# Eight changes of order in a hybrid encoder block: masks before gate casts, up casts after the last inverse, x loads after the gates', QKV low parts on VectorE, first MLP blocks in order

## The chip, the cores and the metric

The kernel runs on one core of a Trainium2 chip. A core has a matrix engine (TensorE, PE in the profile), a vector engine (VectorE, DVE), a scalar engine (ScalarE, ACT), a general engine (GpSimd, POOL) and SyncE (SP), which here only issues DMA transfers. Each engine works through its own list of instructions in order, and semaphores tie the lists together. The metric is the device time of one execution, in microseconds (us).

## The reference, cut to what matters

One layer, 1024 tokens, model width 1024, all in float32:

```python
h = rms_norm(x, norm_mix)
proj = h @ w_in                       # 768 columns QKV, 1792 RWKV, 2048 gates
q, k = rotary(rms_norm(q)), rotary(rms_norm(k))
attn = windowed_gqa(q, k, v, sink)    # 8 query heads, 2 key heads, +-128 tokens
rw   = rwkv7_time_mix(shifted(zr))    # a forward and a backward scan, summed
gates = sigmoid(proj[..., O_GATE:])   # one gate per branch and channel
merged = gates[0] * (attn @ w_up_attn) + gates[1] * (rw @ w_up_rwkv)
x = x + merged @ w_out
x = x + square(relu(rms_norm(x) @ w_ff1)) @ w_ff2
x = x + (p @ w_ple) * sigmoid(rms_norm(x) @ w_ple_gate)
```

The scan updates, for each of 8 heads and both directions, a 64 x 64 state at every token: `state * w + (state @ a) b^T + v k^T`, and reads it with `r`.

## The kernel before, in words

**Operands.** Every float32 operand of a large product is split in two by `split` (L196): a high part, cast by ScalarE (L201), and a low part, the remainder, by VectorE or GpSimd (L202). A product is then three matmuls: high by high, high by low, low by high. A weight block therefore goes through a load into a staging buffer, a cast and a subtraction before TensorE can use it. `load_w` (L213) does this for a block of 128 columns, here in two parts of 128x512.

**Order.** A planner gives each engine's instructions their order, from the program's order as a priority and its own simulation of when operands are there. `tc.keep_in_program_order` pins an instruction to the program's order; the helper `mmo` (L228) does so for a matmul and `turn` for VectorE's instructions of the recurrence. `after(ins, prev)` asks for one instruction to stand behind another on its engine.

**Stages.** First come the norm of x and the QKV projection, a token tile of 128 at a time. The eight weight rows of QKV are loaded and split by `load_wq`; the tuple `WQP` names those whose low part GpSimd makes, the others are VectorE's. `rotated(t)` (from L417 on) normalises and rotates queries and keys of a tile and casts them (L433, L438), and `heads(t)` transposes them (L404) and copies the result out of PSUM with ScalarE (`qkT`, L406). The heads of the last two tiles, `h6` and `h7`, are spread among the matmuls of the projection's next blocks.

Then come attention, the RWKV projections and half of the gates. The scan works in chunks of 64 tokens, 16 steps `s`, both directions at once. A step masks products of the chunk's operands (`gm`, L1192, by VectorE), solves with the inverse of a triangular matrix, and carries the state on. The inverses are made for a block of NB = 4 steps at a time while the steps of the block before it run: `inverse_steps` has 31 pairs of VectorE instructions (L1324, L1327) and a last turn with two transposes, `Zn` and `Zt` (L1331, L1332). A step takes as many of these 32 turns as the row of `TURNS` for its place in the block says, in three positions. `end_inverse` joins the quarter blocks at the end of every fourth step: TensorE's `qps` matmuls, ScalarE's copies `Q` and `zi` (L883, L884).

TensorE has gaps in a scan step, and the generator `beside` fills them: it yields one matmul at a time, of the gates of the second half of the tokens, then, after 16 empty yields (`BRIDGE`), of the lift of the attention branch (`uaps`). `fill(n)` takes n of them. What the generator emits between two yields, loads and splits among it, stands in the program where its step is taken. Before the lift it casts two weight blocks and four parts of the attention's output (`wuhi`, `aTh`). In the last `end_inverse`, behind step 11, the generator's steps are taken between the first and the second half of the `qps` matmuls, by `between`, and at once after.

Behind the scan the RWKV branch is lifted (`up_rwkv`, 8 blocks for each half of the tokens). For each block SyncE loads a gate tile `g1t` and the gated attention part `mgt`, and the next up weights, and at places of its list parts of `w_out` (`load_wo`) and the tiles of x. In the code before, four tiles of x (`x1a`) and the gain row `gainf` have no order asked for but the program's.

The output projection, the second norm and the MLP follow. The MLP multiplies in blocks with seven products each, whose operands are sums of blocks (`product`, L1664). Its first two row blocks (`p` of 0 and 1) begin before all of the sums are made. These matmuls are placed by the planner.

Of the kernel before, what the change touches and what calls it, by code (L numbers as in the profile page):

```python
# [17 lines left out]
P = 128  # L18
# [27 lines left out]
NAT = (0, 1)  # L46
WQP = (0, 2, 4)
WQPIN = 8
# [18 lines left out]
FILLQ = (9, 7)  # L67
TURNS = ((0, 0, 4), (3, 2, 5), (3, 2, 5), (4, 3, 1))

LOW_AT = (1, 2)  # L70
# [77 lines left out]
def block_kernel(ctx: ExitStack, tc: tile.TileContext, I: dict, out: bass.AP):  # L148
# [63 lines left out]

    def load_w(pl, tag, src, n, bufs=2, sbufs=2, lo_eng=None, stag=None, parts=1, stages=(), q=None):  # L213

        k = src.shape[1]
        hi = pl.tile([P, k, n], F32R, name="whi", tag=tag + "_hi", bufs=bufs)
        lo = pl.tile([P, k, n], F32R, name="wlo", tag=tag + "_lo", bufs=bufs)
        step = k // parts
        for i in range(0, k, step):
            spl, stg, sb = stages[(i // step) % len(stages)] if stages else (pl, stag or tag + "_st", sbufs)  # L220
            st = spl.tile([P, step, n], F32, name="wst", tag=stg, bufs=sb)
            (q or nc.sync).dma_start(st, src[:, i:i + step])
            split(hi[:, i:i + step], lo[:, i:i + step], st, lo_eng or nc.gpsimd)
        return hi, lo
# [103 lines left out]
    def gates(h, ms=range(2 * KT), mm=nc.tensor.matmul, lo_of=lambda m: nc.gpsimd):  # L328

        for m in ms:  # L330
            c0 = O_GATE + m * P
            hi, lo = load_w(PW, "w", w_col(c0), P, parts=2, lo_eng=lo_of(m), q=nc.gpsimd if (h, m) in GQ else None)
            ps = PMM.tile([P, 512], F32, name="gmm", tag="mm", bufs=2)
            yield from mm3_steps(ps, [(hi[:, k, :], lo[:, k, :], Hh[h][:, k, :], Hl[h][:, k, :]) for k in range(KT)], mm)
            th = PW.tile([P, 512], F32, name="gth", tag="gth", bufs=2)
            nc.scalar.activation(out=th, in_=ps, func=AF.Tanh, scale=0.5)
            epi["stored"] = nc.sync.dma_start(g_d[m, :, 512 * h:512 * h + 512], th)
            yield
# [4 lines left out]
    with ExitStack() as s0:  # L343
# [141 lines left out]
        for h in range(2):  # L485
            ps = PMM.tile([P, 512], F32, name="mm", tag="mm", bufs=2)
            z12.append(ps)
            for i, _ in enumerate(mm3_steps(ps, [(whl[0][:, k, :], whl[1][:, k, :], Hh[h][:, k, :], Hl[h][:, k, :]) for k in range(KT)])):
                if i % 6 == H6[0] and h == H6[1]:
                    next(h6, None)  # L490
            if h == 0:
                if H6[1] == 0:
                    for _ in h6:
                        pass
                rotated(NT - 1)
        for _ in h6:
            pass
        whl = load_w(PW, "w", w_col(O_RWKV + 1664), P, parts=2)
        z13 = []
# [504 lines left out]
    def beside():  # L1004
# [40 lines left out]

        ahead = [weights(0, sts[0])]
        for k in range(NP):
            part(k)
        load_at(1)
        ahead.append(weights(1, sts[1]))  # L1050
        for _ in range(BRIDGE):
            yield 1
# [123 lines left out]
    def products(s, hf):  # L1176
# [14 lines left out]
        for e in range(2):  # L1191
            turn(nc.vector.tensor_tensor(  # L1192
                out=gm[hf][:, s % NB, e].rearrange("p (a b) t -> p a b t", b=2), in0=pss[e][:, 0:6].rearrange("p (a b) t -> p a b t", b=2),
                in1=gmask.unsqueeze(2).broadcast_to([P, 3, 2, 64]), op=ALU.mult))

    def load_v(s):
# [180 lines left out]
    for s in range(NCH):  # L1377
# [28 lines left out]
        aside(0)  # L1406
        inverse_turn(TURNS[s % NB][0])
        gap(1)
# [3 lines left out]
        if more:  # L1412
            products(s + 2, 1)
        inverse_turn(TURNS[s % NB][1])
        gap(2)
# [7 lines left out]
        if first:  # L1423
            inv[0] = inverse_steps(s // NB + 1)
        inverse_turn(TURNS[s % NB][2])
        gap(5)
# [4 lines left out]
        if s % NB == NB - 1 and s // NB < 3:  # L1431
            end_inverse(s // NB + 1, lambda: fill(FILLQ[0]))
            fill(FILLQ[1])
        if s % NB or s // NB >= 3:
# [28 lines left out]
    def load_wo(n, ks, spl, tag, sbufs):  # L1463

        for k in ks:
            st = spl.tile([P, 2, 512], F32, name="wst", tag=tag, bufs=sbufs)
            nc.sync.dma_start(st, wov[:, k:k + 2, 512 * n:512 * n + 512])
            split(wo[n][0][:, k:k + 2], wo[n][1][:, k:k + 2], st, behind=None if n else epi["done"])

# [3 lines left out]
    for e in range(2):  # L1473
        mTh[e] = AC[e].tile([P, KT, 512], F32R, name=f"mh{e}", tag="ab0", bufs=1)
        mTl[e] = AC[e].tile([P, KT, 512], F32R, name=f"ml{e}", tag="ab1", bufs=1)

    def up_rwkv(m, e):

# [3 lines left out]
        mg = GP.tile([P, 2, 256], F32, name="mgt", bufs=3)  # L1482
        nc.sync.dma_start(mg, tset(mg_d[m], e))
        if (m + e) % 2:
# [74 lines left out]
    with ExitStack() as s7:  # L1559
# [14 lines left out]
        gainf = NR.tile([P, DM], F32, name="gainf", bufs=1)  # L1574
        nc.sync.dma_start(gainf, I["gains"][1:2, :].partition_broadcast(P))
        for i in (4, 5, 6, 7, 0, 1, 2, 3):
            t = torder[i]
            nc.sync.dma_start(x1[t], I["x"][t * P:(t + 1) * P, :])
            out_proj(i, 0)
# [78 lines left out]
    def product(ps, p, r, start=True):  # L1658
# [3 lines left out]
        for k in range(4):  # L1662
            for i, (x_, y_) in enumerate(((ah, bh), (ah, bl), (al, bh))):
                nc.tensor.matmul(ps, x_[:, k, :], y_[:, k, :], start=start and k + i == 0, stop=k == 3 and i == 2, skip_group_check=True)  # L1664

# [369 lines left out]
```

## Time and profile before

| what | value |
| --- | --- |
| median of 3 runs | 1653.21 us (1650.28 to 1654.63) |
| the profiled execution | 1652.3 us |
| its span in the profile | 1650.5 us, 31173 instructions |
| TensorE busy | 1601.0 us, 97% |
| VectorE busy | 1136.0 us, 69% |
| ScalarE busy | 840.0 us, 51% |
| GpSimd busy | 90.6 us, 5% |
| mean granted TensorE clock | 0.992 of full speed |

Times in the views are microseconds from the start of the span. A row of the timeline has start, duration, engine, source line, operation, output and inputs, shapes and a count; in brackets stands the idle time of the engine ahead of it and what ended that. A row of the waits has who waited and for whom, then the total, the number of times and the longest. A row of windows has the stretch, its length, each engine's busy time with a count of instructions (PE, PEld, DVE, ACT, POOL), the granted clock, the share of time that the DMA engines were busy and what they moved. SPq is SyncE's DMA queue; an SPq row is the issue of a transfer, not the transfer.

### The profile page before, as it was taken

Reading aid. Unit: us, or ns where it says so; the run is one execution under the profiler, and the core shown is the slowest. Engines: PE = TensorE matmul, PEld = TensorE weight load, DVE = VectorE, ACT = ScalarE, POOL = GpSimd, SP = SyncE. Lnnn points to the kernel's source line nnn. Section 1 sums busy time; section 2 is a strip of 40 time slices with the busy share of each in tenths; the row PEclk is TensorE's granted clock in tenths of the full one; section 3 lists DMA queues with packets and bytes.
Section 4 is the critical chain, followed back from the end, with each engine's and each line's share of the span. In section 5 each row is a group of like instructions: output and inputs, shape, how many; then the busy total and the mean of one; then the engine's idle time right before and its main releaser. Section 6 shows DMA issues by size and latency. Waiting matters only on the chain.

```text
span 1650.5 us, 31173 instructions
## 1 busy us (share of the span) xinstructions
PE 1601.0 (97%) x12280; PEld 1297.2 (79%) x12280; DVE 1136.0 (69%) x2071; ACT 840.0 (51%) x1533; POOL 90.6 (5%) x113
## 2 busy tenths in 40 slices
PE   7999999999999999899999999999999999999998
PEld 6987777776678778676788778888888888888887
DVE  5648998468929679787827877666658877675332
ACT  5548888378653554554305454444445445454221
POOL 3430000310000000000001000000000000000000
PEclk9999999999989999999999999999999999999999
DMA  6352555864475744468723254444459855564011
GB/s 224 86 154 83 173 173 178 263 189 141 136 192 175 225 138 149 148 194 268 242 76 116 79 190 141 147 159 149 161 189 336 266 181 180 171 196 143 35 42 39
DMA packets 199810, 269.23 MB, mean 163 GB/s; under 512 B 47728, under 2 KB 103920, under 8 KB 199664
## 3 DMA queue, kind: packets, MB, share of 16 engines
q1 hardware_dynamic: 188448, 249.95, 47.6%
q0 software_dynamic: 11072, 16.78, 3.8%
q8 instruction: 96, 1.57, 0.4%
q10 hardware_dynamic: 144, 0.52, 0.1%
q14 instruction: 50, 0.41, 0.1%
HBM read 186.45 MB, written 80.74 MB: 162 GB/s over the span
## 4 chain that ended last, share of the span: by engine, by line
PE 73%; DVE 9%; DMA 7%; ACT 6%; issue 4%; POOL 1%; SPq 0%; DVEq 0%; POOLq 0%; ACTq 0%
PE ff1ps L1664 16%; PE ff2ps L1916 16%; PE gmm L228 4%; PE plps L238 2%; PE plps L236 2%; PE plps L234 2%; PE mm L246 2%; PE mm L247 2%; PE mm L248 2%; PE mmo L248 1%; PE mmo L246 1%; PE mmo L247 1%; DMA wst<-in_w_col_dram 1%; PE gps L228 1%; PE uaps L228 1%
## 5 line engine op out<-in xcount | busy, mean ns | idle before, releaser
L1916 PE MATMUL ff2ps<-tl,sh 128*128 128x512 f32 x448 | 174.5, 390 | 0.4 <-DVE tl L202 0.4
L1916 PE MATMUL ff2ps<-th,sl 128*128 128x512 f32 x448 | 174.4, 389 | 0.0
L1916 PE MATMUL ff2ps<-th,sh 128*128 128x512 f32 x448 | 173.9, 389 | 0.0
L201 ACT CAST sh<-sst 128x512 fp32r<-128x512 f32 x109 | 67.8, 622 | 101.5 <-PE ff2ps L1916 46.3
L202 DVE TENSOR_TENSOR sl<-sst,sh 128x512 fp32r<-128x512 f32 x109 | 75.0, 688 | 46.4 <-ACT sh L201 46.1
L1664 PE MATMUL ff1ps<-mh,w1h 128*128 128x512 f32 x256 | 100.3, 392 | 2.0 <-ACT w1h L201 2.0
L1664 PE MATMUL ff1ps<-ml,w1h 128*128 128x512 f32 x256 | 99.9, 390 | 0.0
L1664 PE MATMUL ff1ps<-mh,w1l 128*128 128x512 f32 x256 | 99.6, 390 | 0.0
L1916 PEld LDWEIGHTS ff2ps<-tl,sh 128*128 128x128 f32 x448 | 84.1, 188 | 18.6 <-DVE tl L202 1.1
L201 ACT CAST whi<-wst 128x512 fp32r<-128x512 f32 x100 | 60.0, 618 | 75.3 <-DMA wst<-in_w_col_dram 31.9
L1916 PEld LDWEIGHTS ff2ps<-th,sh 128*128 128x128 f32 x448 | 84.0, 188 | 17.9 <-ACT th L201 0.3
L1916 PEld LDWEIGHTS ff2ps<-th,sl 128*128 128x128 f32 x448 | 84.1, 188 | 17.4
L201 ACT CAST w1h<-w1st 128x512 fp32r<-128x512 f32 x48 | 28.4, 620 | 105.5 <-DMA w1st<-in_w_ff_dram 66.0
L202 DVE TENSOR_TENSOR wlo<-wst,whi 128x512 fp32r<-128x512 f32 x88 | 58.7, 684 | 19.7 <-ACT whi L201 17.0
L185 POOL TENSOR_TENSOR rstd<-ms,neghalf 128x1 f32<-128x1 f32 x24 | 14.8, 616 | 1016.0 <-PE ff2ps L1916 573.4
L202 DVE TENSOR_TENSOR w1l<-w1st,w1h 128x512 fp32r<-128x512 f32 x48 | 31.7, 687 | 50.4 <-ACT w1h L201 50.4
L1664 PEld LDWEIGHTS ff1ps<-mh,w1h 128*128 128x128 f32 x256 | 48.1, 188 | 13.0 <-ACT w1h L201 2.9
L1664 PEld LDWEIGHTS ff1ps<-mh,w1l 128*128 128x128 f32 x256 | 48.1, 188 | 11.0 <-DVE w1l L202 0.9
L1664 PEld LDWEIGHTS ff1ps<-ml,w1h 128*128 128x128 f32 x256 | 48.1, 188 | 10.0
L1192 DVE TENSOR_TENSOR gm<-gps,gmask 128x384 f32<-128x384 f32 x64 | 32.6, 549 | 32.7 <-PE gps L228 32.7
L234 PE MATMUL gmm<-hh,whi 128*128 128x512 f32 x128 | 52.2, 408 | 2.1 <-ACT whi L201 2.1
L228 PE MATMUL gmm<-hh,wlo 128*128 128x512 f32 x128 | 54.2, 423 | 0.0
(406 smaller groups left out, 4508.6 us busy)
## 6 DMA issues: line engine op xcount, KB each, us to landing
tst<-in_w_ff_dram SPq DMA_DIRECT2D x80, 256.0 KB, 4.1
wst<-in_w_col_dram SPq DMA_DIRECT2D x76, 256.0 KB, 3.8
w1st<-in_w_ff_dram SPq DMA_DIRECT2D x32, 512.0 KB, 5.0
hid_S<-h SPq DMA_DIRECT2D x64, 256.0 KB, 2.1
sst<-hid_S SPq DMA_DIRECT2D x64, 256.0 KB, 3.3
hid_A<-h SPq DMA_DIRECT2D x48, 256.0 KB, 2.0
sst<-hid_A SPq DMA_DIRECT2D x45, 256.0 KB, 3.7
ra_d<-ra SPq DMA_DIRECT2D x8, 1024.0 KB, 6.4
```

The lines of the kernel that those rows point to most:

```text
L201: a = nc.scalar.copy(hi, src)
L202: b = (lo_eng or nc.vector).tensor_tensor(out=lo, in0=src, in1=hi.bitcast(F32), op=ALU.subtract)
L228: tc.keep_in_program_order(nc.tensor.matmul(*a, **kw))
L234: mm(ps, ah, bh, start=(i == 0), stop=False)
L236: mm(ps, ah, bl, start=False, stop=False)
L238: mm(ps, al, bh, start=False, stop=(i == n - 1))
L246: nc.tensor.matmul(ps, ah, bh, start=(i == 0), stop=False)
L247: nc.tensor.matmul(ps, ah, bl, start=False, stop=False)
L248: nc.tensor.matmul(ps, al, bh, start=False, stop=(i == n - 1))
L1192: turn(nc.vector.tensor_tensor(out=gm[hf][:, s % NB, e].rearrange("p (a b) t -> p a b t", b=2), in0=pss[e][:, 0:6].rearrange("p (a b) t -> ...
L1664: nc.tensor.matmul(ps, x_[:, k, :], y_[:, k, :], start=start and k + i == 0, stop=k == 3 and i == 2, skip_group_check=True)
L1916: nc.tensor.matmul(banks[bs][i], x_[:, isl], y_, start=fresh and p + j == 0, stop=p == NPR - 1 and j == 2, skip_group_check=True)
```

## The change

Eight edits, none of which adds or takes away a matmul:

1. `WQP` is emptied: VectorE makes all low parts of QKV weights.
2. A second table `TURNS2` sets the inverse's turns in steps 8 to 11. It has the same sum, with the last turn taken earlier in step 11.
3. The casts ahead of the attention's lift are traced once `epi["turned"]` is set, which is behind the last `end_inverse`; the number of empty yields stays 16, or more if that is later.
4. The low part of gate block 1 of the second half is ordered behind the mask products of `products(0, 1)`.
5. `rotated(NT - 1)` is traced behind all of tile 6's heads.
6. `load_wo` splits each row of a weight part alone (128x512 instead of 128x1024).
7. The first four x loads are each ordered behind one of the last four loads of `mgt`, the rest behind the x load before; `gainf` is loaded behind the last of them.
8. The matmuls of the first two row blocks of the MLP are pinned to the program's order.

```diff
-WQP = (0, 2, 4)
+WQP = ()
 TURNS = ((0, 0, 4), (3, 2, 5), (3, 2, 5), (4, 3, 1))
+TURNS2 = ((0, 0, 5), (3, 3, 5), (3, 3, 5), (4, 1, 0))
...
-            split(hi[:, i:i + step], lo[:, i:i + step], st, lo_eng or nc.gpsimd)
+            split(hi[:, i:i + step], lo[:, i:i + step], st, lo_eng or nc.gpsimd, behind=(None, behind))
...
+            hi, lo = load_w(PW, "w", w_col(c0), P, parts=2, lo_eng=lo_of(m), q=nc.gpsimd if (h, m) in GQ else None,
+                            behind=epi.get("gm") if (h, m) == (1, 1) else None)
...
-                rotated(NT - 1)
         for _ in h6:
             pass
+        rotated(NT - 1)
...
-        ahead = [weights(0, sts[0])]
-        for k in range(NP):
-            part(k)
-        load_at(1)
-        ahead.append(weights(1, sts[1]))
-        for _ in range(BRIDGE):
+        n = 0
+        while n < BRIDGE or "turned" not in epi:
+            if "turned" in epi and "parts" not in epi:
+                ahead = [weights(0, sts[0])]
+                for k in range(NP):
+                    part(k)
+                load_at(1)
+                ahead.append(weights(1, sts[1]))
+                epi["parts"] = True
+            n += 1
             yield 1
...
         for e in range(2):
-            turn(nc.vector.tensor_tensor(
+            a = (nc.vector.tensor_tensor(
...
+            turn(a)
+            if s == 0:
+                epi["gm"] = a
...
-        inverse_turn(TURNS[s % NB][0])
+        inverse_turn((TURNS2 if s // NB == 2 else TURNS)[s % NB][0])
...
             end_inverse(s // NB + 1, lambda: fill(FILLQ[0]))
+            if s // NB == 2:
+                epi["turned"] = True
             fill(FILLQ[1])
...
-            split(wo[n][0][:, k:k + 2], wo[n][1][:, k:k + 2], st, behind=None if n else epi["done"])
+            for j in range(2):
+                split(wo[n][0][:, k + j], wo[n][1][:, k + j], st[:, j], behind=None if n else epi["done"])
...
-        nc.sync.dma_start(mg, tset(mg_d[m], e))
+        upl.append(nc.sync.dma_start(mg, tset(mg_d[m], e)))
...
-        nc.sync.dma_start(gainf, I["gains"][1:2, :].partition_broadcast(P))
-        for i in (4, 5, 6, 7, 0, 1, 2, 3):
+        for j, i in enumerate((4, 5, 6, 7, 0, 1, 2, 3)):
             t = torder[i]
-            nc.sync.dma_start(x1[t], I["x"][t * P:(t + 1) * P, :])
+            a = nc.sync.dma_start(x1[t], I["x"][t * P:(t + 1) * P, :])
+            after(a, upl[12 + j] if j < 4 else xload)
+            xload = a
+            if i == 0:
+                after(nc.sync.dma_start(gainf, I["gains"][1:2, :].partition_broadcast(P)), upl[15])
...
-                nc.tensor.matmul(ps, x_[:, k, :], y_[:, k, :], start=start and k + i == 0, stop=k == 3 and i == 2, skip_group_check=True)
+                (mmo if p < 2 else nc.tensor.matmul)(ps, x_[:, k, :], y_[:, k, :], start=start and k + i == 0, stop=k == 3 and i == 2, skip_group_check=True)
```

More of the change, by code (lines that the diff above doesn't have):

```diff
@@ L211, in split, with load_w @@
         return a, b
-    def load_w(pl, tag, src, n, bufs=2, sbufs=2, lo_eng=None, stag=None, parts=1, stages=(), q=None):
+    def load_w(pl, tag, src, n, bufs=2, sbufs=2, lo_eng=None, stag=None, parts=1, stages=(), q=None, behind=None):
         k = src.shape[1]
@@ L331, in gates @@
             c0 = O_GATE + m * P
-            hi, lo = load_w(PW, "w", w_col(c0), P, parts=2, lo_eng=lo_of(m), q=nc.gpsimd if (h, m) in GQ else None)
+            hi, lo = load_w(PW, "w", w_col(c0), P, parts=2, lo_eng=lo_of(m), q=nc.gpsimd if (h, m) in GQ else None,
+                            behind=epi.get("gm") if (h, m) == (1, 1) else None)
             ps = PMM.tile([P, 512], F32, name="gmm", tag="mm", bufs=2)
@@ L1413, in block_kernel @@
             products(s + 2, 1)
-        inverse_turn(TURNS[s % NB][1])
+        inverse_turn((TURNS2 if s // NB == 2 else TURNS)[s % NB][1])
         gap(2)
@@ L1424, in block_kernel @@
             inv[0] = inverse_steps(s // NB + 1)
-        inverse_turn(TURNS[s % NB][2])
+        inverse_turn((TURNS2 if s // NB == 2 else TURNS)[s % NB][2])
         gap(5)
@@ L1475, in block_kernel @@
         mTl[e] = AC[e].tile([P, KT, 512], F32R, name=f"ml{e}", tag="ab1", bufs=1)
+    upl = []
     def up_rwkv(m, e):
```

## The prediction, made before the changed kernel was run

> **What bounds the kernel now.** I read the head of the page first, then the list of TensorE's waits, then the granted clock by stretches of the span, and last the order of time around each place that the diff touches.
>
> ```profile
> span 1650.5 us, 31173 instructions
> PE 1601.0 (97%) x12280; PEld 1297.2 (79%) x12280; DVE 1136.0 (69%) x2071; ACT 840.0 (51%) x1533; POOL 90.6 (5%) x113
> ...
> PE gps L228 <- DVE gm L1192: 3.0, 1, 3.0
> PE gps L228 <- ACT zi L884: 2.9, 1, 2.9
> PE mmc L248 <- DVE wlo L202: 1.8, 2, 0.9
> PE ff1ps L1664 <- ACT w1h L201: 2.0, 2, 1.5
> PE qtp L404 <- ACT qkT L406: 1.6, 1, 1.6
> ```
>
> TensorE is busy for 1601.0 of 1650.5 us, and the change takes no matmul away. So it can win only single waits (columns: total us, times, longest) and time in which TensorE ran at a lower clock, which the busy share hides. The next rows (start:end, us; busy us and count of PE, PEld, DVE, ACT, POOL; granted clock; DMA share; GB/s) show three such stretches, each behind one of those waits.
>
> ```profile
> 453.00:460.00 7.00, 6.08 (x46) 5.21 (x47) 2.35 (x5) 1.04 (x3) 0.54 (x1) 0.51 1.23 243
> 668.00:671.50 3.50, 3.50 (x84) 2.48 (x86) 2.75 (x5) 2.91 (x5) 0.00 (x0) 0.51 0.02 5
> 678.00:681.70 3.70, 3.70 (x85) 2.83 (x80) 3.70 (x9) 2.37 (x5) 0.00 (x0) 0.54 0.94 286
> ```
>
> Work of 6.08 us at a clock of 0.51 would take 3.1 at full clock: 2.9 us are lost there. In the same way 3.50 x 0.49 = 1.7 and 3.70 x 0.46 = 1.7. So a wait of 1.5 to 3.0 us costs about twice its length when such a stretch follows.
>
> **Start: QKV low parts by VectorE.**
>
> ```profile
> 8.79 2.34 POOL L202 TENSOR_TENSOR wql<-wqs,wqh 128x768 fp32r<-128x768 f32 x1 [0.78 <-ACT wqh L201]
> 11.16 0.33 SPq L355 DMA_DIRECT2D wqs<-in_w_qkv_dram  x1
> 11.37 0.96 DVE L202 TENSOR_TENSOR wql<-wqs,wqh 128x768 fp32r<-128x768 f32 x1
> 20.67 1.80 ACT L201 CAST wqh<-wqs 128x768 fp32r<-128x768 f32 x2 [3.70 <-DMA wqs<-in_w_qkv_dram]
> 22.55 0.44 PE L460 MATMUL psq<-wql,hh 128*128 128x384 f32 x1 [0.55 <-DVE wql L202]
> ```
>
> A low part takes POOL 2.34 us and VectorE 0.96. POOL ends the first at 11.13, and SyncE issues the next load into that staging buffer at 11.16. VectorE would do it behind its work of that moment, and I estimate the load 0.65 earlier. The last weights reach TensorE at 22.55, after 3.70 us of ScalarE's waiting for DMA, so an earlier load can show there. Bounds: 0 (the queue is full of x and weights, and POOL's three parts, 2.9 us of VectorE, delay a norm there) to 1.4 (2.34 - 0.96). I take **0.65**.
>
> **The last query/key tile behind the heads of the tile before it.**
>
> ```profile
> 106.99 0.62 ACT L433 CAST q<-qn 128x512 fp32r<-128x512 f32 x1 [6.10 <-DVE qn L430]
> 107.91 1.06 ACT L406 CAST qkT<-qtp 128x512 fp32r<-128x512 f32 x2
> 108.54 0.66 PE L404 MATMUL qtp<-ident,k 128*128 128x128 f32 x4 [1.58 <-ACT qkT L406]
> ...
> 108.50:112.00 3.50, 3.46 (x20) 2.92 (x20) 0.92 (x4) 2.21 (x4) 1.89 (x3) 1.00 0.60 167
> ```
>
> ScalarE stands 6.10 us in front of tile 7's q cast, and the eviction that TensorE wants is queued behind it, to 107.91. With `rotated(7)` traced last, that eviction no longer has the cast in front. The clock behind this gap stays at 1.00, so nothing is added for it. Bounds 0 (tile 7's heads, a block of matmuls later, come late instead: their q cast moves behind all of tile 6's evictions) to 1.58. I take **1.6**.
>
> **The gates' low part behind the masks (block 1 of half 1).**
>
> ```profile
> 449.22 1.38 DVE L873 COPY zi<-Zt 32x1024 f32<-32x1024 f32 x2
> 451.20 0.69 DVE L202 TENSOR_TENSOR wlo<-wst,whi 128x512 fp32r<-128x512 f32 x1 [0.60 <-ACT whi L201]
> 452.71 0.69 DVE L202 TENSOR_TENSOR wlo<-wst,whi 128x512 fp32r<-128x512 f32 x1 [0.81 <-ACT whi L201]
> 453.32 1.01 DVE L1192 TENSOR_TENSOR gm<-gps,gmask 128x384 f32<-128x384 f32 x2
> 453.92 2.01 PE L228 MATMUL gps<-rac,bkc 64*64 64x128 f32 x32 [3.03 <-DVE gm L1192]
> ```
>
> VectorE is free at 449.22 + 1.38 = 450.60, yet it stands in two low parts that wait for their casts, and the masks start 2.7 us later. Put first, the two masks run to about 451.6 and the low parts follow; TensorE still stands about 0.7, so the wait falls by 2.3, and the stretch behind it regains 2.9: **5.2**, bounds 2.0 (clock kept low, the low part then late for its gate block) and 5.9 (all of 3.03 and 2.9). What the added order holds back are the two low parts, and behind them the gate block's matmuls; these wait for the masks at most their 1.0 us.
>
> **More inverse steps early, and casts behind the last inverse.**
>
> ```profile
> 630.72 0.32 DVE L1327 TENSOR_TENSOR Z<-Z,tmp 128x156 f32<-128x156 f32 x1
> ...
> 664.00 2.13 DVE L1331 STREAM_TRANSPOSE Zn<-Z 128x1024 f32<-128x1024 f32 x1
> 665.95 2.06 DVE L1332 STREAM_TRANSPOSE Zt<-Z 128x1024 f32<-128x1024 f32 x1
> 666.28 1.28 PE L228 MATMUL qps<-Zn,lt 32*32 32x32 f32 x128 [1.47 <-DVE Zn L1331]
> 673.84 0.61 ACT L201 CAST wuhi<-wust 128x512 fp32r<-128x512 f32 x1
> 674.36 2.17 ACT L201 CAST aTh<-gm 128x512 fp32r<-128x512 f32 x4
> 676.44 0.61 ACT L201 CAST wuhi<-wust 128x512 fp32r<-128x512 f32 x1
> 677.07 0.58 ACT L884 COPY zi<-qps 32x512 f32<-32x512 f32 x1
> ```
>
> Step 11 now does 5 of the 32 turns rather than 8 and ends with the transposes inside the step, so the wait for Zn (1.47) and its half-clock stretch (1.7) go. The last zi copy stands behind six casts (673.84 to 677.07, 3.2 us); traced after it, they free the wait for zi (2.9) and its stretch (1.7). Together 7.8. What is late next: the six casts, all ready at once, go in front of the evictions of step 12's chain on ScalarE. As one queue they cost at most their own 3.2 us, at least 0; I take the 3.2, since each step has such an eviction. The three turns moved to steps 8 to 10 add one pair each, 2 x 0.32 us.
>
> ```profile
> 628.00:641.50 13.50, 13.40 (x292) 11.01 (x291) 12.95 (x36) 4.45 (x8) 0.00 (x0) 1.00 0.50 156
> ```
>
> VectorE is busy for 12.95 of 13.50 us there, so 0.55 of 0.64 fits; bounds 0 to 1.9 over three steps, I take 0.3 as 3 x 0.09. Net **4.3**; bounds 1.0 (no clock back: 1.47 + 2.9 - 3.2 - 0.3, about 0.9) and 7.8.
>
> **The x loads and the finer w_out parts.**
>
> ```profile
> 773.10 1.28 SPq L1578 DMA_DIRECT2D x1a<-in_x_dram  x3
> 790.65 0.62 ACT L201 CAST whi<-wst 128x512 fp32r<-128x512 f32 x1 [0.80 <-DMA wst<-in_w_up_rwkv_dram]
> 811.88 0.32 SPq L1483 DMA_DIRECT2D mgt<-mg_d  x1
> ...
> 775.00:800.00 25.00, 24.12 (x107) 19.61 (x106) 21.89 (x32) 10.27 (x16) 0.00 (x0) 1.00 0.89 289
> 825.00:850.00 25.00, 25.00 (x112) 20.71 (x111) 5.71 (x7) 2.10 (x2) 0.00 (x0) 1.00 0.24 85
> ...
> L1572 DVE SCALAR_TENSOR_TENSOR x1a<-mmo,x1a x8: 685/692/692, 844.0 to 885.0; 128x512 f32<-128x512 f32 x8
> ```
>
> Four x loads of half a megabyte stand ahead of the gates' and the lifted products' loads on SyncE's queue; DMA is 0.89 busy to 800, and a cast waits for an up weight. The new edges put the x loads behind the last four mg loads, which end at 811.88, and the x tile is first read at 844.0, with DMA 0.24 busy ahead of it: the move is hidden. The 128x1024 parts become two each, and the half parts let an up weight's low part between them. The two waits of 0.9 are what can go: **1.5**, bounds 0 (weights late for another reason) to 1.8. `gainf` moves behind too and is hidden likewise.
>
> **First MLP blocks in order.**
>
> ```profile
> 931.58 0.50 PE L1664 MATMUL ff1ps<-mh,w1h 128*128 128x512 f32 x1 [1.51 <-ACT w1h L201]
> ```
>
> The first two row blocks' products keep program order, so the matmuls that need a late w1h no longer stand in front of others whose operands were there. **1.5** of the 2.0 in the waits' list, bounds -0.5 (a pinned matmul now waits for its own weight) to 2.0.
>
> **The sum** is 0.65 + 1.6 + 5.2 + 4.3 + 1.5 + 1.5 = 14.75. Most stages of the kernel are ordered by a planner, and each edit changes what it sees from that place on; I take 15% off, an estimate, since a wait that goes is often met again in part: 12.5. The span becomes 1638.0. The profiled run was 1652.3, 1.8 above its span, and the runs' median of 1653.2 is 0.9 above that: 1638.0 + 1.8 + 0.9 = **1641**.
>
> [...]
>
> **The rivals.**
> *A: the waits go, the clock stays low.* If the half-clock stretches come at their places for another reason than the gap ahead, 6.3 is not won: 14.75 - 6.3 = 8.5, less 15%, 7.2, so 1646. For it speaks that the 1.58 us gap near 107 has a clock of 1.00 behind it; against it that all three lie right behind a gap.
> *B: the waits move.* The last casts hold step 12, tile 7's heads come late, and the low parts wait for the same weights: about half the sum, 6, so 1648 and up.
> *C: slower, VectorE becomes the bound of steps 8 to 11.* Its three extra pairs (1.9) and the two transposes (4.2) then stand in the state's chain, the six casts behind them (3.2), and each of the four steps opens a gap that halves the clock for 3.5 us (4 x 1.7): 16.1 lost, against 0.85 x 10.45 = 8.9 won elsewhere: 7 slower, 1660. It decides once the pairs and transposes (6.1) are met by two such stretches (3.4). VectorE's 12.95 of 13.50 speaks for it, 0.55 free per step and a step 11 with fewer turns against it.
> *D: nothing changes.* The planner already puts the casts, loads and matmuls where the change would, or other late data sets the same ends: 1652. The waits listed by name speak against.
>
> **How the numbers follow.** Forecast 0.52 (1636 to 1644), A 0.14, B 0.14, C 0.08, D 0.12. About 0.3%, 5 us, can be told from no change. Faster: forecast, A and half of B, 0.73; same: half of B and D, 0.19; slower: C, 0.08. Low end: the upper bounds 1.4 + 1.6 + 5.9 + 7.8 + 1.8 + 2.0 = 20.5, so 1633. High end 1651, which leaves out C and D.
>
> **What would show it.** Right: the gaps behind gm, zi, Zn, qkT and w1h gone or under 1 us, a clock near 1.00 at 445 to 455 and 655 to 680, x loads issued past 800, six casts behind the last zi copy. Wrong: gaps of over 1.5 us at new names in 440 to 700, evictions of UV behind wuhi and aTh casts, VectorE above 13.3 per step, or the low clock without a gap ahead.

## The result

The changed kernel takes 1644.82 us, the median of 20 runs (1641.69 to 1648.57); the kernel before, run beside it 20 times, takes 1651.75 (1645.70 to 1658.05). The ratio is 0.9960 with a 95% interval of 0.9949 to 0.9971: faster by 0.4%, 6.9 us between the medians. The forecast was 1641 and 12 us, the range 1633 to 1651. The direction and the range hold; the gain is a little over half of the forecast's.

The profiled execution took 1642.74 us with a span of 1641.0, so 9.5 us less span than before. 2.6 of these 9.5 are the choice of execution: this one lies 2.1 below its median, the profiled one of before lies 0.5 above its own.

These are the head of the page after and the first of TensorE's waits (total us, times, longest).

```profile
span 1641.0 us, 31193 instructions
PE 1595.3 (97%) x12280; PEld 1294.0 (79%) x12280; DVE 1134.7 (69%) x2082; ACT 841.3 (51%) x1541; POOL 83.4 (5%) x110
```

```profile
PE wy L229 <- issue: 4.3, 3, 3.6
PE wa L229 <- issue: 2.4, 2, 1.8
PE uaps L229 <- DVE gta L1073: 2.2, 2, 1.5
PE ff1ps L229 <- DVE u L1766: 2.1, 1, 2.1
PE qtp L406 <- ACT qkT L408: 1.9, 1, 1.9
```

The waits for gm (3.0), for zi (2.9) and for Zn (1.5) are gone from the head of the list, as forecast. In their place stand gaps with no releaser ("issue"): 3.6 us at `wy` and 1.8 at `wa`. The wait for qkT is still there, and the MLP waits for a vector sum `u` instead of for `w1h`. Busy time fell by 5.7 us without a matmul less, and the stretches at half clock (leaving out the first 30 us and the last few) fell from 23.9 us in six places to 10.2 in two. Windows of the changed kernel's profile, read like those above:

```profile
445.00:455.00 10.00, 9.62 (x221) 7.38 (x213) 4.71 (x9) 4.85 (x9) 1.08 (x2) 1.00 1.13 299
455.00:460.00 5.00, 3.19 (x69) 2.51 (x68) 1.02 (x2) 1.17 (x3) 0.00 (x0) 1.00 1.03 292
...
665.50:672.50 7.00, 5.21 (x119) 4.34 (x122) 6.01 (x12) 5.46 (x11) 0.00 (x0) 0.52 0.50 159
921.50:925.00 3.50, 3.49 (x9) 2.78 (x10) 1.16 (x2) 0.33 (x1) 0.00 (x0) 0.52 0.34 109
```

Half clock now stands in 6.8 us at the end of step 11 (665.5 to 672.3) and in 3.4 us in the MLP; before, it stood at 306, 453, 477, 668, 678 and 764.

Where the time went shows best by marks that both programs have. The table gives, from the start of one instruction to the start of another, the stage's time in the two profiles, and the spread over the profiles below that keep the edits of that stage. "Masks of chunk n" are the `gm` multiplies for chunk n, which run in step n - 2; the expectations below call the same marks "step n".

| stage | forecast won | before | after | won | other profiles with the edit |
| --- | --- | --- | --- | --- | --- |
| to the last QKV matmul | 0.65 | 96.20 | 93.08 | 3.1 | 93.0 to 94.5 |
| on to the last qtp transpose of the heads | 1.6 | 19.38 | 19.66 | -0.3 | 19.3 to 21.2 |
| last attention score to masks of chunk 1 | 5.2 | 32.36 | 28.90 | 3.5 | 28.1 to 29.9 |
| masks of chunk 8 to chunk 15 | 4.3 | 121.10 | 120.76 | 0.3 | 120.3 to 122.5 |
| last mean of the epilogue to the last uaps | none | 14.15 | 11.62 | 2.5 | 11.3 to 11.9 |
| first to last matmul of the RWKV lift | 1.5 | 46.13 | 45.71 | 0.4 | 45.6 to 46.4 |
| MLP matmuls 48 to 96 | 1.5 | 12.81 | 14.99 | -2.2 | 13.4 to 15.0 |

The rows add up to 7.3 of the 9.5 us. The six that were forecast add up to 4.8 of the 14.75 that were forecast for them; 2.5 come from a stage that was not.

### The profile page after: what moved, and what is told of

It reads as the page before. It is cut to its first block, busy times and chain, and to the rows that moved or that the text cites. A ratio compares the mean times of both kernels' runs of the same rounds, so it can differ in the third digit from the quotient of the medians.

```text
span 1641.0 us, 31193 instructions
## 1 busy us (share of the span) xinstructions
PE 1595.3 (97%) x12280; PEld 1294.0 (79%) x12280; DVE 1134.7 (69%) x2082; ACT 841.3 (51%) x1541; POOL 83.4 (5%) x110
## 4 chain that ended last, share of the span: by engine, by line
PE 73%; DVE 13%; ACT 5%; DMA 5%; issue 3%; POOL 1%; SPq 0%; DVEq 0%; ACTq 0%; POOLq 0%
PE ff2ps L1933 19%; PE ff1ps L1681 16%; PE gmm L229 2%; DMA wst<-in_w_col_dram 2%; PE plps L239 2%; PE plps L237 2%; PE plps L235 2%; PE mm L247 2%; PE mm L248 2%; PE mm L249 2%; DVE Z L1336 2%; DVE tmp L1333 1%; PE mmo L248 1%; PE mmo L247 1%; PE mmo L249 1%
## 5 line engine op out<-in xcount | busy, mean ns | idle before, releaser
L1681 PE MATMUL ff1ps<-mh,w1h 128*128 128x512 f32 x224 | 87.5, 391 | 0.4 <-ACT w1h L202 0.4
L1681 PE MATMUL ff1ps<-ml,w1h 128*128 128x512 f32 x224 | 87.4, 390 | 0.0
L1681 PE MATMUL ff1ps<-mh,w1l 128*128 128x512 f32 x224 | 87.2, 389 | 0.0
L203 DVE TENSOR_TENSOR w1l<-ssum,w1h 128x512 fp32r<-128x512 f32 x64 | 43.1, 689 | 14.4 <-ACT w1h L202 14.4
L229 PE MATMUL gmm<-hh,wlo 128*128 128x512 f32 x128 | 52.8, 412 | 0.0
L235 PE MATMUL gmm<-hh,whi 128*128 128x512 f32 x128 | 51.5, 402 | 0.9 <-ACT whi L202 0.9
L229 PE MATMUL gmm<-hh,whi 128*128 128x512 f32 x128 | 52.4, 409 | 0.0
L239 PE MATMUL gmm<-hh,wlo 128*128 128x512 f32 x128 | 51.6, 403 | 0.6 <-POOL wlo L203 0.5
```

The lines of the kernel that those rows point to most:

```text
L203: b = (lo_eng or nc.vector).tensor_tensor(out=lo, in0=src, in1=hi.bitcast(F32), op=ALU.subtract)
L229: tc.keep_in_program_order(nc.tensor.matmul(*a, **kw))
L235: mm(ps, ah, bh, start=(i == 0), stop=False)
L239: mm(ps, al, bh, start=False, stop=(i == n - 1))
L1681: (mmo if p < 2 else nc.tensor.matmul)(ps, x_[:, k, :], y_[:, k, :], start=start and k + i == 0, stop=k == 3 and i == 2, skip_group_check= ...
```

## The experiments

Each kernel below is the changed one with one edit more or less. Where a kernel was timed repeatedly, a ratio is given; of the others only the stages are used, since single times of one program differ by 7 us. The stages of those come from one profile each.

**The changed kernel again, unaltered.**

> The changed kernel once more, unaltered, to see which of its gaps belong to the program and which to one execution. If the gaps come from order and queues, the 3.6 us before the fourth wy matmul behind step 11, the 2.1 us before the first T3h matmul of the MLP, the 1.9 us before the last qtp of tile 6 and the 1.8 us among the wa matmuls near 455 are all there within 0.5 us. If the instruction-side gaps (no releaser shown) are an accident of one execution, the first and the last of these differ by over 1 us. The half-clock stretches may come at other places in either case; the time lies between 1641 and 1649.

Its span was 1643.5. The four gaps stand at the same instructions: 3.87 us at `wy`, 1.37 at `wa`, 1.59 at the qtp and 2.14 at `u`. All are within 0.5 us of the first profile (`wa` by 0.44), so they belong to the program. Half clock does not: it stood at 465.5 to 472.5 and 667 to 674, and not behind the MLP's gap, although that gap was 2.14 us in both. In ten profiles with this MLP gap of 2.1 us the half-clock stretch followed it six times and four times not; that alone is 1.6 us of a run, and shows in the last row of the table as 13.4 or 15.0. Where the gap falls in time goes with it. In the clock rows of the kernel before's trace (13 changes) and of the changed kernel's (5) any two changes lie a whole multiple of 3.413 us apart: the stretches last 3.413, 6.827, 17.067, 143.36 us and so on. The windows of nine other profiles, which show two changes or more, agree. Counted from the span's start this grid lies at 2.45 us in the first trace and at 3.26 in the second. In the six, TensorE was busy for 37 to 40% of the grid's stretch that held most of the gap; in the four, a border of the grid split the gap, and the emptier stretch was busy for 51 to 57%. From 30 to 1600 us of the two traces, each of the 6 stretches at full clock with under 46% busy was followed by half clock, 2 of the 19 with 46 to 78%, and none of the 883 with more.

**What the gaps with no releaser are.** TensorE's order around the 3.6 us gap, in the changed kernel:

```profile
663.36 0.33 PE L229 MATMUL wy<-rac,Sc 64*64 64x64 f32 x4
667.29 1.01 PE L229 MATMUL wy<-rac,Sc 64*64 64x64 f32 x27 [3.60 <-issue]
```

The gap falls among matmuls of one kind after the fourth, and the profile shows no releaser that the fifth waited for. The trace also has a queue that it marks "instruction" (q8 on the page): 96 transfers of 16384 bytes, where TensorE has 24760 instructions in the changed kernel and 24758 in the one before, so one transfer to 258. I call these transfers blocks. Set against them, with TensorE's loads, matmuls and semaphore instructions numbered in order of their starts:

```
kernel            instruction  256 earlier  last before  block arrives    resumes  after landing
before                  14786       670.55       672.19  671.04 to 672.00  673.37       1.37
changed                  5057       451.57       455.52  454.73 to 455.89  457.54       1.65
changed                 14785       662.18       663.47  664.88 to 665.84  667.29       1.44
changed again           14785       664.49       665.77  667.56 to 668.48  669.87       1.38
sge loads later         14785       665.98       667.26  667.64 to 668.56  669.98       1.42
512 KB copy added       14785       662.05       663.34  663.80 to 665.20  666.61       1.41
old turns               14786       662.74       664.03  663.82 to 664.78  666.16       1.38
```

In the profiles of the kernel before and of the changed one, every gap of over 0.5 us with no releaser behind 440 us, 5 and 6 of them, stands at an instruction whose number is 193 or 194 over a multiple of 256, and ends 1.25 to 1.65 us after such a block has landed. The two traces also pair blocks and numbers in order: the first block starts within 5.0 us before or 3.5 us after TensorE's start at number 193, the second at number 449, and so on to the last, and TensorE starts the number 256 further never sooner than 1.25 us after the block has landed. That fits a TensorE that has run out of instructions; it is my reading, since the profile names no releaser. The second half of the `qps` work is 128 matmuls of 32 x 32 with 128 weight loads, 256 instructions, and TensorE is through 256 in 1.29 us here (662.18 to 663.47), while the next block took 0.96 us of transfer and 1.44 more until TensorE went on, after the 2.70 us until its transfer started. In the kernel before, part of that work ran at half clock (the stretch 668.00 to 671.50) and took 1.64 us, and TensorE went on 1.2 us after its last instruction instead of 3.8. Only 0.35 of these 2.6 us is the slower work; the other 2.2 are the transfer, which started 0.49 us after the boundary where it started 2.70 after it in the changed kernel.

Among the long matmuls of these two profiles, behind 740 us, no such gap of over 0.5 us stands, and TensorE comes to the next boundary 24.6 to 35.4 us after the block for it has landed. Among the small ones of the scan a gap of 4.15 us stands at a boundary in the kernel with edit 3 undone, below.

**Are data loads what delays the block?** Two 256 KB loads start in front of it. In the first kernel they go behind the last load of the attention's second half, kept as `epi["at_load"]`; in the second a copy is added behind them for the first half of the epilogue.

```diff
-            nc.sync.dma_start(epi["sg"][:, 1], I["g2"])
+            after(nc.sync.dma_start(epi["sg"][:, 1], I["g2"]), epi["at_load"])
...
-        nc.sync.dma_start(sge, tset(sg_d, e))
+        after(nc.sync.dma_start(sge, tset(sg_d, e)), epi["at_load"])
```

> Only the two 256 KB loads of sge move on SyncE's queue, behind the four loads of the attention's second half; every engine's own order is the same. Fetch theory: the 3.6 us gap among the wy matmuls is a wait for TensorE's next block of instructions (16 KB, landing at 665.8 in the changed kernel, after 5.1 us instead of 3.7 before), held up by these loads; without them the block is asked for at the same place and lands 1 to 2 us earlier, the gap falls to 1 to 2 us and the half-clock stretch at 665.5 to 672.5 is shortened or gone: 2 to 5 us won on the stage up to step 13. Rival (the gap is a wait for the casts, for zi or for a result that the profile does not name): the gap stays at 3.6 within 0.3 us, since none of these moved.

```diff
-        nc.sync.dma_start(sge, tset(sg_d, e))
+        a = nc.sync.dma_start(sge, tset(sg_d, e))
+        if e == 0:
+            after(nc.sync.dma_start(x1_d[0:P, :], I["x"][0:P, :]), a)
```

> A copy of 512 KB of x from memory to memory is added behind the two sge loads (its target is written anew later); the rest is unaltered. Fetch theory: the block lands later by about the time of the added 512 KB read and write, 2 to 3 us at 350 GB/s, so the gap among the wy matmuls grows from 3.6 to 5 us or more. Rival (a wait on an engine's result): the gap stays at 3.6.

TensorE's timeline behind the gap, in the kernel with the later loads and then in the one with the added copy:

```profile
669.98 0.51 PE L229 MATMUL wy<-rac,Sc 64*64 64x64 f32 x13 [2.50 <-issue]
```

```profile
666.61 0.70 PE L229 MATMUL wy<-rac,Sc 64*64 64x64 f32 x17 [3.05 <-issue]
```

With the loads later the gap falls from 3.60 and 3.87 to 2.50 us, not to the 1 to 2 that were expected: the block starts 1.66 us after the boundary where it started 2.7 and 3.1 after. With 512 KB more it did not grow to 5 but stood at 3.05: that expectation failed. (For its 350 GB/s: the changed kernel's DMA engines moved 256 to 420 GB/s in slices of 0.2 us from 663.0 to 664.8.) Ten profiles with the new turns and the loads where they were, the added copy's among them, have gaps of 3.05 to 4.15, so the loads may be a part of 0.5 to 1.7 us, and one profile is all that shows it; with the old turns the later loads came with 1.59 instead of 1.91. So the gap's end goes with the landing of a block, 1.37 to 1.65 us behind it in the seven rows; what decides when its transfer starts (0.5 to 3.2 us after the boundary) stays open. In time the later loads gave a ratio of 0.9954 to the kernel before (0.9939 to 0.9969), the same as the changed kernel's.

**Edits 2 and 3, one at a time.**

```diff
-        inverse_turn((TURNS2 if s // NB == 2 else TURNS)[s % NB][0])
+        inverse_turn(TURNS[s % NB][0])
...
```

> The changed kernel with the first table of turns in steps 8 to 11 too (edit 2 undone, the casts still behind the last inverse). Theory: TensorE's instruction supply, not Zn, bounds the end of step 11. In six profiles every gap with no releaser stands at an instruction whose number is 193 or 194 over a multiple of 256, 1.25 to 1.65 us behind the landing of a 16 KB block. Then the wait for Zn comes back (about 1.5 us), the gap among the wy matmuls falls from 3.6 to 3.9 us to about 2 us or less, the wait of 0.9 us for W in step 11 and the 0.8 us lost up to step 12 go, and the time at step 14 is equal or up to 2 us earlier than in the changed kernel. Rival (edit 2 wins the Zn wait as the prediction had it): the Zn wait and its half clock come back, the wy gap stays, and step 14 is 2 to 3 us later.

TensorE's timeline in this kernel:

```profile
658.51 1.28 PE L229 MATMUL qps<-Zn,lt 32*32 32x32 f32 x128 [1.46 <-DVE Zn L1340]
...
666.16 1.01 PE L229 MATMUL wy<-rac,Sc 64*64 64x64 f32 x26 [1.91 <-issue]
```

The wait for Zn came back with 1.46 us, and the gap for the block went from 3.60 to 1.91: what one gives the other takes. A wait of TensorE for W, 0.8 us in the changed kernel, is gone too: from the masks of chunk 10 to those of chunk 12 the new turns take 1.4 to 1.5 us longer than the kernel before in each profile that has them, the old turns the same as before. Chunks 8 to 15 take 120.91 us against 120.76 and 120.76 in the two profiles with the new turns. So edit 2 won nothing that can be seen; the median of four runs was 1642.62, ratio 0.9943 (0.9925 to 0.9961).

```diff
+        ahead = [weights(0, sts[0])]
+        for k in range(NP):
+            part(k)
+        load_at(1)
+        ahead.append(weights(1, sts[1]))
+        for _ in range(BRIDGE):
+            yield 1
```

(in place of the loop that waits for `epi["turned"]`)

> The changed kernel with the up casts traced where they were (edit 3 undone, the new turns kept). Theory: the six casts go ahead of the last zi copy again and TensorE stands about 3 us for zi before the gps matmuls of step 12; the wy gap for the instruction block is still there at about 3.5 us (the block is asked for when TensorE reaches the block before), so step 14 is about 3 us later than in the changed kernel. Rival: waiting for zi and waiting for the block overlap, and step 14 is within 1 us of the changed kernel.

Only one instruction changes its place on ScalarE: the last zi copy is again behind the six casts. ScalarE's rows, then TensorE's:

```profile
666.78 0.61 ACT L202 CAST wuhi<-wust 128x512 fp32r<-128x512 f32 x1
667.30 2.17 ACT L202 CAST aTh<-gm 128x512 fp32r<-128x512 f32 x4
669.38 0.61 ACT L202 CAST wuhi<-wust 128x512 fp32r<-128x512 f32 x1
670.02 0.57 ACT L886 COPY zi<-qps 32x512 f32<-32x512 f32 x1
```

```profile
669.50 1.01 PE L229 MATMUL wy<-rac,Sc 64*64 64x64 f32 x27 [4.15 <-issue]
670.21 0.32 PE L229 MATMUL wy<-Sc,rac 64*64 64x64 f32 x2
...
671.06 0.44 PE L229 MATMUL gps<-rac,bkc 64*64 64x128 f32 x2
```

The zi copy ends at 670.59, late as before, and nobody waits: TensorE stood at the boundary until 669.50 and reaches `gps` at 671.06. The rival held: the two waits overlap, and from the masks of chunk 13 to those of chunk 14 it takes 22.27 us against 22.02 in the changed kernel. Edit 3 took away a wait that the gap at the boundary would have covered. Chunks 8 to 15 take 121.68 us, within the 120.3 to 122.5 of the profiles that keep the edit.

**Edit 4: the masks.**

```diff
-                            behind=epi.get("gm") if (h, m) == (1, 1) else None)
+                            behind=None)
```

> The changed kernel without the order of gate block 1's low parts behind the masks (edit 4 undone); on VectorE only these two instructions go back ahead of four masks, nothing else moves. Theory: the 3.0 us wait for gm comes back and the 1.3 to 1.9 us gap for an instruction block among the wa matmuls, which is 256 instructions long before its landing, falls below 0.5 us, since the block comes while TensorE waits; a half-clock stretch stands behind the wait. Step 1 is then 1 to 4 us later, and the clear effect of the edit is 1.5 us plus the clock, not 5.2. Rival: the block's gap stays at 1.3 to 1.9 too, and step 1 is 5 us later, as the prediction had it.

VectorE and TensorE in the changed kernel, then in the one with the edit undone:

```profile
446.55 1.02 DVE L1198 TENSOR_TENSOR gm<-gps,gmask 128x384 f32<-128x384 f32 x2
447.16 1.35 PE L229 MATMUL gps<-rac,bkc 64*64 64x128 f32 x32 [0.35 <-DVE gm L1198]
457.54 0.63 PE L229 MATMUL wa<-UV,gm 64*64 64x64 f32 x15 [1.81 <-issue]
```

```profile
450.37 0.69 DVE L203 TENSOR_TENSOR wlo<-wst,whi 128x512 fp32r<-128x512 f32 x1 [0.43 <-ACT whi L202]
450.98 1.01 DVE L1198 TENSOR_TENSOR gm<-gps,gmask 128x384 f32<-128x384 f32 x2
...
451.58 1.35 PE L229 MATMUL gps<-rac,bkc 64*64 64x128 f32 x32 [2.80 <-DVE gm L1198]
462.80 0.63 PE L229 MATMUL wa<-UV,gm 64*64 64x64 f32 x15 [1.24 <-issue]
```

The wait is 2.80 us without the edit and 0.35 with it. The block's gap was not the other side of it, as my theory had it: it is 1.24 without the edit and 1.1 to 1.9 with it. The stage from the last score to the masks of chunk 1 takes 32.18 us against 28.1 to 29.9. So this edit won 2.3 to 4.1 us; the rival's 5 was too much: only 3.4 us of half clock came back where before 6.8 stood, and the gap at `wa` (in the kernel before, the two instructions start 0.35 us apart) is new in all of them.

**Edit 5, asked for by name.** In the changed kernel ScalarE stands as it did before, 6.12 us in front of tile 7's cast with two evictions behind it:

```profile
104.16 0.62 ACT L435 CAST q<-qn 128x512 fp32r<-128x512 f32 x1 [6.12 <-DVE qn L432]
104.68 0.50 ACT L440 CAST k<-qn 128x128 fp32r<-128x128 f32 x2
105.08 1.06 ACT L408 CAST qkT<-qtp 128x512 fp32r<-128x512 f32 x2
```

```diff
-                nc.scalar.copy(qkT, tp)
+                epi["qkT"] = nc.scalar.copy(qkT, tp)
...
-            nc.scalar.copy(q2[:, :, 0, :], qn[:, 0:NH])
+            a = nc.scalar.copy(q2[:, :, 0, :], qn[:, 0:NH])
+            if t == NT - 1:
+                after(a, epi["qkT"])
...
-                nc.scalar.copy(k4[:, :, 0, j, :], kt)
+                a = nc.scalar.copy(k4[:, :, 0, j, :], kt)
+                if t == NT - 1:
+                    after(a, epi["qkT"])
```

> The q and k casts of tile 7 are ordered behind the last eviction of tile 6's heads on ScalarE; nothing else moves. Theory: edit 5 moved the program's order only, and the planner put the casts where they had been (107.0 before and 104.2 after, 6.1 us of standing in both); with the order asked for, the 1.9 us gap before tile 6's last qtp is gone and the stage up to the last qtp gets 1.6 to 2.0 us shorter. Rival (tile 7's heads then come late, or the PSUM tile is the limit): a gap of over 1 us stands at a qtp of tile 7, and less than 0.5 us is won.

ScalarE's timeline of this kernel, and a window of it:

```profile
103.67 0.59 ACT L408 CAST qkT<-qtp 128x512 fp32r<-128x512 f32 x1 [1.24 <-PE qtp L406]
105.49 0.59 ACT L408 CAST qkT<-qtp 128x512 fp32r<-128x512 f32 x1 [1.24 <-PE qtp L406]
105.98 0.62 ACT L435 CAST q<-qn 128x512 fp32r<-128x512 f32 x1
```

```profile
104.00:108.00 4.00, 4.00 (x22) 3.24 (x21) 2.37 (x10) 2.76 (x7) 1.25 (x2) 1.00 0.52 147
```

TensorE is busy without a gap and the stage from the last QKV matmul to the last qtp takes 17.59 us against 19.66 and 19.40: 1.8 to 2.1 won, and 17.59 again in the last kernel below, which has this order too. The mechanism was right, the edit did not bring it about: it moved the program's order, and the planner's order stayed.

**Edit 1.**

```diff
-WQP = ()
+WQP = (0, 2, 4)
```

> The changed kernel with GpSimd making three of the QKV low parts again (edit 1 undone). Theory: the 1.7 to 3.2 us won up to the last QKV matmul come from this edit alone, so it ends at 96 us again, within 0.7 us of the kernel before. Rival (the start varies from one execution to the next, or another edit's order sets it): it ends at 93 to 95 us as in the profiles with the edit.

The last QKV matmul starts at 97.80, against 93.0 to 94.5 with the edit: nothing of the 1.7 to 3.2 us (against 96.20) is left without it, so they are this edit's. The expected 0.7 us around 96.20 was missed by 0.9; a half-clock stretch at 22.70 to 26.11, which the kernel before does not have, costs 1.7 us of it. VectorE's rows of the kernel before, then of the changed one:

```profile
13.32 4.49 DVE L202 TENSOR_TENSOR wql<-wqs,wqh 128x768 fp32r<-128x768 f32 x2 [0.39 <-ACT wqh L201]
18.55 1.29 DVE L261 SCALAR_TENSOR_TENSOR xs<-xt,rstd,gain 128x1024 f32<-128x1024 f32 x1 [0.67 <-POOL rstd L185]
```

```profile
12.70 3.56 DVE L203 TENSOR_TENSOR wql<-wqs,wqh 128x768 fp32r<-128x768 f32 x4
16.99 1.29 DVE L262 SCALAR_TENSOR_TENSOR xs<-xt,rstd,gain 128x1024 f32<-128x1024 f32 x1 [0.67 <-POOL rstd L186]
17.28 1.74 ACT L202 CAST wqh<-wqs 128x768 fp32r<-128x768 f32 x2 [1.41 <-DMA wqs<-in_w_qkv_dram]
```

Beside GpSimd's low parts (12.63 to 16.99) VectorE needed 4.49 us for two of its own, 2.25 each; with edit 1 undone, beside GpSimd's again, two take 4.50. In the changed kernel, with GpSimd idle, four take 3.56, 0.89 each. So VectorE makes four in less time than it had taken for two, the second tile's norm starts 1.6 us earlier (its x load is issued at 6.27 where it was at 11.53, behind the sixth weight), and the last weights' casts start at 17.28 where they had started at 20.67. What the two engines share there is not shown.

**Edits 6 and 7 undone** (the x loads, `gainf` and the 128x1024 parts as in the first diff's minus lines).

> The changed kernel with the x loads, gainf and the 128x1024 parts of w_out as they were (edits 6 and 7 undone). Theory: the lift of the RWKV branch takes 46.1 us from its first to its last matmul in the kernel before and 45.6 to 46.4 us in nine profiles with the edits, so they won nothing there, and without them it is 46 to 47 us; the stage from the last mups to the last uaps, 14.2 us before and 11.3 to 11.8 in these profiles, stays near 11.5. Rival (the x loads held up the stage ahead too): that stage goes back to about 14 us, or the lift to over 47.

The one gap that TensorE has in the lift then:

```profile
798.19 0.50 PE L249 MATMUL mmc<-rwh,wlo 128*128 128x512 f32 x1 [2.03 <-DVE wlo L203]
```

The lift takes 49.47 us, against 45.6 to 46.4 with the edits and 46.13 in the kernel before: the rival's "over 47" came. One weight is 2.03 us late, and a short half-clock stretch follows. So against the kernel before the two edits won nothing that is clear of the spread, yet beside the other edits the one profile without them is 3 us longer. Which of the moved loads or parts makes that weight late stays open. The stage ahead stays at 11.64, so its gain is not theirs.

**Edit 8, undone and mended.**

```diff
-                (mmo if p < 2 else nc.tensor.matmul)(ps, x_[:, k, :], y_[:, k, :], start=start and k + i == 0, stop=k == 3 and i == 2, skip_group_check=True)
+                nc.tensor.matmul(ps, x_[:, k, :], y_[:, k, :], start=start and k + i == 0, stop=k == 3 and i == 2, skip_group_check=True)
```

> The changed kernel with the MLP's first matmuls left to the planner (edit 8 undone). Theory: pinning only took away four matmuls that had filled the same wait for u; unpinned, the gap is 1.5 us before a matmul that waits for w1h, and the stage from the 48th to the 96th MLP matmul is 1 to 2.5 us shorter than in the changed kernel. Rival (the pinning won 1.5 us, as the prediction had it): that stage is 1 to 2 us longer.

```diff
-            s_ = tmp("u2")
+            s_ = tmp("u3")
```

> One buffer name is changed in the changed kernel: the sum ahead of the first two blocks' squared ReLU lies in u3, unused at that time, and not in u2. Theory: the 2.1 us gap before the first T3h matmul is a wait for the vector sum u that reads the PSUM bank which T3 adds to; u itself stands behind ScalarE's reading of the shared u2 buffer and three other vector instructions. With its own buffer it can run near 918 to 919, the gap falls below 0.5 us, and the half-clock stretch behind it goes: 2 to 4 us won between the 48th and the 96th MLP matmul. Rival (T3's and T4's operands or weights are what is late): the gap stays over 1.5 us.

The first matmul of the MLP's third sum in the changed kernel, in the one with edit 8 undone (where another matmul, which waits for w1h, stands at this place), and in the one with the other buffer:

```profile
921.51 0.80 PE L229 MATMUL ff1ps<-T3h,w1h 128*128 128x512 f32 x1 [2.14 <-DVE u L1766]
```

```profile
923.04 0.50 PE L1681 MATMUL ff1ps<-mh,w1h 128*128 128x512 f32 x1 [1.51 <-ACT w1h L202]
```

```profile
921.27 0.47 PE L229 MATMUL ff1ps<-T3h,w1h 128*128 128x512 f32 x1 [0.41 <-ACT w1h L202]
```

Undone, matmuls 48 to 96 take 12.82 us, as before the change (12.81), against 13.4 to 15.0 with the edit: it costs 0.6 us, and 2.2 when half clock follows. With a buffer of its own the sum `u` starts at 920.45, 5.5 us after the stage's start where it started 7.3 after it, with the matmuls of the stage in the same order. TensorE waits 0.41 us, and the stage takes 11.68: 1.1 less than before, 1.7 to 3.3 less than in the changed kernel. Some of it is given back at once, 0.86 us before a later matmul at 945.37. Ratio 0.9946 (0.9928 to 0.9964), median of four runs 1642.29.

**All together**: tile 7's casts ordered, the sge loads later, the u3 buffer, the old turns.

> The changed kernel with four alterations: tile 7's casts behind tile 6's last eviction, the sge loads behind the attention's second half, the MLP's first sum in its own buffer, and the first table of turns throughout. Theory: the four gains add up, 1.8 us at the start, 2 to 3 in the MLP and 1 to 2 around the end of step 11, so 4 to 7 us below the changed kernel's median of 1644.8: 1638 to 1641, a ratio of about 0.992 to the kernel before. Rival (what is won in one stage is met by instruction blocks, weights or the clock in the next): within 2 us of the changed kernel.

The median of six runs is 1641.51, the ratio 0.9943 (0.9927 to 0.9959). It is below the changed kernel's 0.9960 (0.9949 to 0.9971), but the intervals overlap. In the stages the gains came: 17.59 us for the heads, 11.65 in the MLP, a block gap of 1.59. But its profile (span 1642.8) has five half-clock stretches of 3.4 us ahead of the tail, in which work lost 8.5 us, where the changed kernel's two lost 4.2. The theory's 4 to 7 us were not shown; 3.3 between the medians were, not clear of the spread, and the kernel before took 1650.04 beside these runs where it took 1651.75 beside the changed one's.

## Why the prediction was right, and where it was not

The time came out inside the range, but by luck more than by the terms: of the six, only the masks came near their size by the mechanism named for them.

- **Start, 0.65.** Mis-sized: 1.7 to 3.2, above my upper bound of 1.4; the 0.65 itself was not worked out from a row. I priced GpSimd's part against VectorE's alone and took VectorE's own parts as they stood; the row with two of them in 4.49 us shows the price that running beside GpSimd's put on them (2.25 us each against 0.89), and on the norm and the load behind them.
- **Last q/k tile, 1.6.** Wrong step: "that eviction no longer has the cast in front". The planner kept ScalarE's order, and the gap was 1.87 us. It was rival D for this one edit; with the order asked for, 1.8 to 2.1 came.
- **Masks, 5.2.** Right mechanism, mis-sized: the wait fell by 2.7 where I had 2.3, the whole won 2.3 to 4.1. What I did not see is late next: the block of instructions, 1.1 to 1.9 us, at `wa`.
- **Turns and casts, 4.3.** Wrong step: "the wait for Zn and its stretch go ... free the wait for zi and its stretch". Both waits went, and nothing was won (0.3, spread -1.4 to 0.8). The gap of 3.6 us at an instruction block's boundary took their place, and 2.5 us that the work behind it lost at half clock; the 1 us gap of before at this place ("issue: 2.0, 3, 1.0" in the waits) has no term in the prediction. The casts did not hold step 12 up, since TensorE does not wait for UV before 711, so the 3.2 that I set against the gain for them is not what took it. VectorE's turns cost 1.5 us up to the masks of chunk 12, where I had 0.3.
- **x loads, 1.5.** Mis-sized: 0.4, spread -0.3 to 0.6 against before. Of the two waits of 0.9 us for a low part one is left in the profiled execution, with 0.41, and in most of the others, with 0.4 to 0.8.
- **MLP, 1.5.** Wrong sign. The step "matmuls that need a late w1h no longer stand in front of others whose operands were there" is false: the others' operands were there, their PSUM tile `ff1ps` was not (2.14 us of waiting), since `u` had yet to read it. Pinning took away four matmuls that had filled the same wait.
- **Not forecast:** the end of the attention's lift takes 2.5 us less in the changed kernel and 2.3 to 2.9 less in the others run here; the wait for gta there went from 2.36 to 1.53, and the other 1.7 is the half-clock stretch of 763.62 to 767.03 that followed it in the one profile of the kernel before. No kernel here brought either back, so they belong to no single edit that was undone, and whether other executions of the kernel before have that stretch is open.
- **Clock.** Rival A said that the half-clock stretches might not go. They went from places and came at others; gaps of 2.1 us were followed by one in six profiles of ten. The prediction priced each stretch as belonging to its wait, where the same wait of 2.1 us has it or not, six times to four, by its place on the grid of 3.413 us.

In all the mechanism was nearer to rival B, waits that move, than to the forecast; one of the prediction's own signs of being wrong came, gaps of over 1.5 us at new names between 440 and 700 (`wy` 3.60, `wa` 1.81). The time, 1644.8, lies just above the forecast's own 1636 to 1644, and the gain of 6.9 us between A's 7.2 and B's 6. The sum came right to a factor of two because a start that was priced too low and 2.5 us that were not forecast stood against a scan and an MLP that were priced too high. C, VectorE as the bound, came only in small: a wait of 0.8 us for W and 1.5 us over two steps.

## What to carry to other kernels

Before a wait is priced as a gain, ask what TensorE would run into next, its own program too: where small matmuls stand dense here, 256 instructions of TensorE were done in 1.3 us, and all 11 gaps of over 0.5 us with no releaser in the profiles of the kernel before and of the changed one stand at a number that repeats over 256 and end 1.25 to 1.65 us behind the landing of an instruction block. A move in the source is a wish where a planner sets the order; look at the engine's list after, or ask for the order by name. A buffer shared by two steps is as good a cause of a wait as data (2.14 us before the MLP's third sum, 0.41 with a buffer of its own); when a product waits, look for who reads its PSUM tile, not only for who writes its operands.

## What was not expected of the hardware

TensorE stood for up to 4.15 us among small matmuls, in the kernel with edit 3 undone, with no releaser in the profile; the seven gaps set against the instruction blocks of 16384 bytes end 1.37 to 1.65 us after one has landed. A subtraction on VectorE took 2.25 us beside GpSimd's and 0.89 alone. And in the traces of the kernel before and of the changed one the clock changes at whole multiples of 3.413 us alone: it halved behind each of the 6 full-clock stretches of that grid in which TensorE was busy for under 46%, and behind none of the 883 with over 78%. So one and the same gap of 2.1 us before the MLP's third sum costs 1.6 us more in one execution than in another (15.0 against 13.4 for matmuls 48 to 96). That is a part of the 7 us by which runs of one program differ.
